# Dilated attention queries and keys kept in token order, with strided operands for the score products

## The chip, the cores and the metric

The kernel runs on one core of one Trainium2 chip. The metric is the device time of one launch in microseconds; three runs of the kernel before the change took 1457.19, 1458.5 and 1459.48 us (median 1458.5). All data is float32. "fp32r" in the profile is a float32 operand that TensorE takes in one pass; a plain float32 product shows as two MATMUL records.

## The reference, cut to what matters

The program is one encoder block: three attention mixers on the same normalised input, gates, and projections. The change touches only the first mixer, a dilated sliding-window attention with 24 heads of 64 in three groups of 8. The groups have dilations 1, 4 and 16:

```python
A_GROUPS = ((128, 1), (512, 4), (2048, 16))      # (window, dilation)
# per group: rope on q and k, then
def regroup(t):                                   # tokens t = u*dilation + r  ->  class r, place u
    return t.reshape(b, L, dilation, h, dh).transpose(0, 2, 1, 3, 4)
sc = einsum('znqhd,znkhd->znhqk', qb, kw) * dh ** -0.5      # within a class only
valid = abs(qpos - kpos) <= half                            # half = 64 places
p = exp(sc - m);  l = sum(p);  o = (p / l) @ v;  lse = m + log(l)
# the three groups' outputs are merged with softmax(lse) over the groups
```

A query sees only keys of its own residue class (token number modulo the dilation), up to 64 places away. In the third group a class has 1024 / 16 = 64 tokens, so it sees its whole class and no band is needed.

## The kernel before, in words

The program works in stages. The one that matters here is the dilated attention, from about 600 to 1030 us of the span. It handles 12 items, one for each pair of heads `p_` (0 to 3) and group `g` (0 to 2), in the order (0,0), (0,1), (0,2), (1,0) and so on.

**Projections.** `add_a` queues two dense units an item, one for the queries and one for the keys. `dense` (lines 143, 145, 147) does a unit as two halves of 512 tokens, 24 matmuls each. `rope_half` empties each half from PSUM: eight quarter multiplications for the rotated part and one full-width one on VectorE (lines 1049 and 1050 through `mult`), and then one addition on GpSimd (line 1056) that writes the rotated queries `aq` or keys `ak`. That addition also sorts: it reads `t1a` and `t2a` through `classes`, with a step of the dilation between elements, and writes through `half_of`, so that `aq` and `ak` hold whole residue classes one after the other.

**Attention of an item.** `scores` (line 1123) multiplies a tile of 128 queries by its window of keys for two heads, which lie on partitions 0 to 63 and 64 to 127. A call does four query tiles. A tile's window of keys has 192 or 256 columns in group 0, 192 in group 1, and 128 in group 2, where a tile holds two classes of 64 one after the other. `soft` adds a mask on VectorE (line 1135) and takes the exponential on ScalarE (lines 1138 to 1143); `trans` transposes on TensorE (lines 1160, 1169) and copies out on ScalarE (line 1172); `pv` (line 1186) multiplies by the values and writes the output `og` in order of tokens on ScalarE (line 1194); `stats` transposes the maxima and sums (line 1205), copies them to `sr` (lines 1208, 1210, 1212) and stores them to `std` in DRAM, for all three groups in the order of 16 classes. `values` loads the item's values from `vdr` into `vfull` (and `vpart`), with SyncE's DMA queue. When the three groups of a pair of heads are done, `combine` reads `std`, forms the weights, sends them through DRAM (`wgd`) and back broadcast (`wgt`), and multiplies `og` by them on VectorE (`weigh`, line 1334), with the sums over groups on GpSimd (line 1338).

**Order.** TensorE's order is written out by hand: `plan` lists the pieces of the current item between those of the last and the next, and `weave` mixes them with the dense matmuls of the item after the next by their costs in nanoseconds. In this stage the order on VectorE, ScalarE, GpSimd and SyncE is found by the framework's scheduler, from dependencies, priorities and its model of costs. Each engine then runs its instructions strictly in that order.

Of the kernel before, what the change touches and what calls it, by code (L numbers as in the profile page):

```python
# [10 lines left out]
AF = mybir.ActivationFunctionType  # L11
OP = mybir.AluOpType
# [3 lines left out]
S = 1024  # L16
# [2 lines left out]
EPS = 1e-6  # L19
HD = 64  # L20
DIL = (1, 4, 16)

C_ID, C_GP, C_GM, C_BM, C_END = 0, 130, 138, 146, 426
B_COS, B_SIN, B_QN, B_QS, B_KN, B_KS = 0, 512, 170, 234, 298, 362
# [26 lines left out]
def block(ctx: ExitStack, tc: tile.TileContext, x, xT, memT, cst, msk, bcst, tabA, gpost,  # L51
          wu, wv, wb, wmem, wbr, wout, out):
    nc = tc.nc
    V, A, G, PE = nc.vector, nc.scalar, nc.gpsimd, nc.tensor
# [390 lines left out]
    for k in range(8):  # L445
        if k % 2 == 0:
            load_wkv(k // 2)
        for e in range(2 if k == 0 else 1):
            t = slice(e * 512, e * 512 + 512) if k == 0 else slice(0, S)
# [206 lines left out]
    half = [slice(0, 512), slice(512, 1024)]  # L656
# [363 lines left out]
    with tc.tile_pool(name="aa", bufs=1, reuse_waits="tile") as aa:  # L1020
# [4 lines left out]
        vpart = aa.tile([P, 8, 2, 64], F32, name="avp")  # L1025
        G.memset(vpart, 0.0)

        def half_of(ap, half, g):

            if g == 0:  # L1030
                return ap[:, half * 512:half * 512 + 512]
            n = S // DIL[g] // 2
            return ap.rearrange("p (r u) -> p r u", r=DIL[g])[:, :, half * n:half * n + n]

        def classes(ap, g):
            return ap if g == 0 else ap.rearrange("p (u r) -> p r u", r=DIL[g])

        OPS = {}

        def rope_half(o, half, p, scale, g):  # L1040

            t = slice(half * 512, half * 512 + 512)
            t1 = ab.tile([P, 512], F32, name="t1a", bufs=3)
            t2 = ab.tile([P, 512], F32, name="t2a", bufs=3)
            cos, sin = tab[0][:, t], tab[1][:, t]

            def mult(out, x, y):
                if scale is None:
                    return V.tensor_tensor(out, x, y, op=OP.mult)  # L1049
                return V.scalar_tensor_tensor(out, x, scale, y, op0=OP.mult, op1=OP.mult)  # L1050

            for a in range(4):
                i, j = slice(32 * a, 32 * a + 32), slice(32 * (a ^ 1), 32 * (a ^ 1) + 32)
                mult(t2[i], p[j], sin[j])
            fp["last"] = mult(t1, p, cos)
            G.tensor_tensor(half_of(o, half, g), classes(t1, g), classes(t2, g), op=OP.add)  # L1056

        def add_a(p_, g):
            base = (p_ * 3 + g) * 2
            d = OPS[p_, g] = {}  # L1060

            def qk_evac(name, scale):
                def evac(half, p):
                    if half == 0:
                        d[name] = ab.tile([P, S], F32, name=f"a{name}", bufs=2)
                    rope_half(d[name], half, p, scale, g)
                return evac

            add_unit(wu[base], qk_evac("q", -0.125))
            add_unit(wu[base + 1], qk_evac("k", None))  # L1070

        def item(p_, g):
# [8 lines left out]
            def values():  # L1081

                v = vdr[g, p_]
                if g == 2:
                    vv = v.rearrange("(u r) f -> u r f", r=16)
                    for z in range(2):
                        nc.sync.dma_start(vfull[z * 64:z * 64 + 64].rearrange("p b h d -> p b (h d)"), vv[:, z::2])
                    return
                if g == 0:
                    nc.sync.dma_start(vfull[:, 0:7].rearrange("p b h d -> p b (h d)"),  # L1090
                                      v[64:960].rearrange("(b q) f -> q b f", q=128))
                else:
                    nc.sync.dma_start(vfull[:, 0:4].rearrange("p b h d -> p b (h d)"),
                                      v.rearrange("(u r) f -> u r f", r=4)[64:192])
                for z in range(2):
                    zs, f = slice(z * 64, z * 64 + 64), slice(z * 64, z * 64 + 64)
                    if g == 0:
                        nc.sync.dma_start(vpart[zs, 0:2, z], v.rearrange("(b q) f -> q b f", q=64)[:, 0::15, f])
                    else:
                        for e in range(2):  # L1100
                            nc.sync.dma_start(vpart[zs, e::2, z], v[768 * e:768 * e + 256].rearrange(
                                "(q r) f -> q r f", r=4)[:, :, f])
# [5 lines left out]
            def scores(b):  # L1108
                if b == 0:
                    d["ops"] = OPS.pop((p_, g))  # L1110
                    d["lx"] = aa.tile([P, 2, NT], F32, name="lxa", bufs=2)
                    d["sts"] = cb.tile([P, 2, 2, NT], F32, name="sts", bufs=2)
                qa, ka = d["ops"]["q"], d["ops"]["k"]
                for j in range(4):
                    T = 4 * b + j
                    lo, hi, _ = window(g, T)
                    n = hi - lo
                    if j % 2 == 0:
                        banks = [pss1(), pss1()]
                    raws[T] = [x[:, j % 2 * 256:j % 2 * 256 + n] for x in banks]  # L1120
                    for h in range(2):
                        hs = slice(h * 64, h * 64 + 64)
                        PE.matmul(raws[T][h], qa[hs, T * 128:T * 128 + 128], ka[hs, lo:hi], start=True, stop=True)  # L1123

            def soft(T):
                lo, hi, mo = window(g, T)
# [48 lines left out]
            def pv(b):  # L1175
                if b == 0:
                    d["og"] = OG[p_, g] = cb.tile([P, S], F32, name="og", bufs=4)
                og = d["og"]
                ov = pst().rearrange("p a b -> p (a b)")
                for j in range(4):  # L1180
                    terms = st.pop(4 * b + j)
                    n = len(terms[0])
                    for i in range(n):
                        for h in range(2):
                            (vt, x), z, pp = terms[h][i]
                            PE.matmul(ov[h * 64:h * 64 + 64, j * 128:j * 128 + 128], vt[:, x, z], pp,  # L1186
                                      start=i == 0, stop=i == n - 1)
                if g == 0:
                    dst, src = og[:, b * 512:b * 512 + 512], ov
                else:  # L1190
                    r = DIL[g] // 2
                    dst = og.rearrange("p (u r) -> p r u", r=DIL[g])[:, b * r:b * r + r]
                    src = ov.rearrange("p (r u) -> p r u", r=r)
                A.activation(dst, src, AF.Copy)

            def stats():
                sts, lx = d["sts"], d["lx"]
                for h in range(2):
                    if g == 1:
                        V.tensor_tensor(sts[:, h, 1, h::2], sts[:, h, 1, h::2], lx[:, h, h::2], op=OP.add)  # L1200
                    elif g == 0:
                        t = slice(7 * h, 7 * h + 1)
                        V.tensor_tensor(sts[:, h, 1, t], sts[:, h, 1, t], lx[:, h, t], op=OP.add)
                tp = pst()
                PE.transpose(tp[0:32, 0, :], sts.rearrange("p h s t -> p (h s t)"), ident)
                sr = cb.tile([32, 128], F32, name="sr", bufs=1)
                if g == 0:
                    A.activation(sr.rearrange("p (b a) -> p b a", b=16), tp[0:32, 0, :].rearrange("p (a b) -> p b a", b=16), AF.Copy)
                elif g == 1:
                    A.activation(sr.rearrange("p (b a) -> p b a", b=4), tp[0:32, 0, :].rearrange("p (a b) -> p b a", b=4), AF.Copy)  # L1210
                else:
                    A.activation(sr, tp[0:32, 0, :], AF.Copy)
                for h in range(2):
                    for q in range(2):
                        row = sr[(h * 2 + q) * 8:(h * 2 + q) * 8 + 8]
                        dst = std[p_, h, g, q]
                        if g == 0:
                            nc.sync.dma_start(dst.rearrange("(b t a) -> t b a", b=16, t=8),
                                              row.rearrange("p (b a) -> p b a", b=16))
                        elif g == 1:  # L1220
                            for f in range(2):
                                nc.sync.dma_start(dst.rearrange("(e r f a) -> f r e a", e=4, r=4, f=2)[f],
                                                  row[f:f + 7:2].rearrange("p (e a) -> p e a", e=4))
                        else:
                            nc.sync.dma_start(dst.rearrange("(t a) -> t a", t=8), row)

            size = [window(g, T)[1] - window(g, T)[0] for T in range(NT)]
            return dict(
# [525 lines left out]
def layout(inp):  # L1754
# [4 lines left out]
    r = {}  # L1759
# [37 lines left out]
    k = np.arange(256)[None]  # L1797
    m = np.zeros((P, 384), f)
    m[:, :256] = np.where(np.abs(p + 64 - k) <= 64, 0.0, 1e30)
    m[:, 256:] = np.where(p // 64 == k[:, :128] // 64, 0.0, 1e30)  # L1800
    r['msk'] = m
    cst[:, C_GP:C_GP + 8] = inp['g_pre'][0].reshape(8, P).T
    cst[:, C_GM:C_GM + 8] = inp['g_mem'][0].reshape(8, P).T
# [53 lines left out]
```

## Time and profile before

| quantity | value |
|---|---|
| median of three runs | 1458.5 us |
| the profiled execution, whole | 1458.88 us |
| its span in the profile | 1457.1 us |
| mean granted TensorE clock | 0.995 |
| TensorE matmul busy (PE) | 1423.2 us, 98% |
| VectorE busy (DVE) | 984.5 us, 68% |
| ScalarE busy (ACT) | 641.8 us, 44% |
| GpSimd busy (POOL) | 499.7 us, 34% |

A row of a group gives line, engine, operation, output<-input, shapes and count, then the busy time, the mean duration in nanoseconds, the idle time of that engine just before, and what ended it. A timeline row gives the start and the duration in microseconds, and in brackets the idle time before and its releaser; neighbouring instructions of a kind stand in one row. The ends of matmuls are modelled and overlap, so the time that a block of matmuls really takes is read from its start to the start of the next row. PEld are TensorE's weight loads. SPq is SyncE's queue.

### The profile page before, as it was taken

To read this page: it belongs to the slowest core of one execution; us is meant where nothing else is said; L and a number is where in the kernel's file an instruction comes from. 1 tells how busy PE (TensorE), PEld (TensorE's weight loads), DVE (VectorE), ACT (ScalarE), POOL (GpSimd) and SP (SyncE) were. 2 spreads that over 40 slices of the span, in tenths; PEclk is the share of its full clock that TensorE was granted. 3 is DMA by queue.
4 is the path that set the end of the run, shared out by engine and by line. 5 is a ranking of instruction groups with operands and counts; after the bars stand their busy time and mean duration, and the time that the engine had idled before them with its cause. 6 is when DMAs were issued, how large, how long until landed. Compare 5 with 4: busy or idle time off the path is not lost.

```text
span 1457.1 us, 20924 instructions
## 1 busy us (share of the span) xinstructions
PE 1423.2 (98%) x7548; PEld 1140.9 (78%) x7548; DVE 984.5 (68%) x1739; ACT 641.8 (44%) x1441; POOL 499.7 (34%) x382
## 2 busy tenths in 40 slices
PE   8999999999999999899999999999999999999998
PEld 7899986565666888687777778778787888888887
DVE  7665468776762367586687686873788787659643
ACT  6543365665554243145444544463534434212221
POOL 1415504666664420132232242230334331035322
PEclk9999999999999999999999999999999999999999
DMA  6332012232112675412131241342443443767122
GB/s 239 100 116 73 17 64 91 80 105 73 62 44 72 237 222 173 122 43 57 47 90 59 57 113 51 89 145 81 139 156 134 173 173 108 272 219 273 48 92 101
DMA packets 99448, 168.05 MB, mean 115 GB/s; under 512 B 21968, under 2 KB 51856, under 8 KB 99344
## 3 DMA queue, kind: packets, MB, share of 16 engines
q1 hardware_dynamic: 80192, 148.76, 31.7%
q10 hardware_dynamic: 19152, 17.96, 3.7%
q8 instruction: 59, 0.97, 0.3%
q14 instruction: 45, 0.37, 0.1%
HBM read 124.38 MB, written 42.30 MB: 114 GB/s over the span
## 4 chain that ended last, share of the span: by engine, by line
PE 76%; DVE 9%; ACT 5%; issue 5%; POOL 3%; DMA 2%; SPq 0%; ACTq 0%; POOLq 0%; DVEq 0%
PE s L125 9%; PE sc L125 9%; PE d L145 9%; PE d L143 8%; PE d L147 8%; PE s L967 6%; PE sc L1705 5%; PE ov L754 3%; PE d L967 2%; PE s L738 2%; PE tr L720 2%; PE s L739 2%; PE d L535 1%; PE tr L1186 1%; PE s L1123 1%
## 5 line engine op out<-in xcount | busy, mean ns | idle before, releaser
L143 PE MATMUL d<-hh,wh 128*128 128x512 f32 x672 | 271.2, 404 | 7.6 <-DVE t1a L1050 5.8
L147 PE MATMUL d<-hh,wl 128*128 128x512 f32 x672 | 269.4, 401 | 0.0
L145 PE MATMUL d<-hl,wh 128*128 128x512 f32 x672 | 269.4, 401 | 0.0
L105 ACT ACTIVATE wh<-wr 128x1024 fp32r<-128x1024 f32 (+1 forms) x79 | 72.2, 917 | 222.1 <-PE d L145 125.8
L143 PEld LDWEIGHTS d<-hh,wh 128*128 128x128 f32 x672 | 127.5, 190 | 38.0 <-issue 10.6
L145 PEld LDWEIGHTS d<-hl,wh 128*128 128x128 f32 x672 | 127.3, 189 | 31.3 <-issue 8.4
L147 PEld LDWEIGHTS d<-hh,wl 128*128 128x128 f32 x672 | 127.4, 190 | 29.1 <-issue 4.7
L745 POOL TENSOR_TENSOR bl<-bl,bp 128x512 f32<-128x512 f32 x96 | 131.5, 1370 | 53.6 <-ACT bp L741 48.1
L125 PE MATMUL sc<-hh,wh 128*128 128x512 f32 x384 | 118.4, 389 | 0.0
L106 DVE TENSOR_TENSOR wl<-wr,wh 128x1024 fp32r<-128x1024 f32 x53 | 74.6, 1409 | 37.5 <-ACT wh L105 37.1
L1056 POOL TENSOR_TENSOR aq<-t1a,t2a 128x512 f32<-128x512 f32 x24 | 44.7, 1862 | 160.7 <-DVE t1a L1050 149.4
L721 DVE TENSOR_REDUCE bn<-tr 128x1 f32<-128x512 f32 x128 | 86.1, 686 | 17.4 <-PE tr L720 16.1
L1049 DVE TENSOR_TENSOR t2a<-d,tab 32x512 f32<-32x512 f32 x96 | 66.0, 687 | 47.2 <-PE d L147 41.9
L741 ACT ACTIVATE bp<-s 128x512 f32<-128x512 f32 x128 | 75.9, 595 | 46.8 <-PE s L739 45.7
L1056 POOL TENSOR_TENSOR ak<-t1a,t2a 128x512 f32<-128x512 f32 x24 | 55.4, 2308 | 117.8 <-DVE t1a L1049 91.9
L125 PEld LDWEIGHTS sc<-hh,wh 128*128 128x128 f32 x384 | 72.1, 188 | 15.0
L1050 DVE SCALAR_TENSOR_TENSOR t2a<-d,tab 32x512 f32<-32x512 f32 x96 | 66.0, 687 | 25.8 <-PE d L147 24.0
L1432 POOL TENSOR_TENSOR sf<-wr 128x512 f32<-128x512 f32 x22 | 29.7, 1368 | 145.1 <-DVE ch L106 71.7
L1636 POOL TENSOR_TENSOR acc<-acc,th 128x1024 f32<-128x1024 f32 x15 | 40.9, 2729 | 112.0 <-DVE th L1635 109.3
L125 PE MATMUL sc<-hl,wh 128*128 128x512 f32 x192 | 74.7, 389 | 0.0
L1143 ACT ACTIVATE pra<-pra,sts 128x128 f32<-128x128 f32 (+2 forms) x152 | 66.4, 438 | 17.0 <-DVE sts L1135 17.0
L1135 DVE CUSTOM_DVE_ANT_0 pra<-s,mask 128x192 f32<-128x192 f32 (+2 forms) x192 | 56.1, 348 | 15.7 <-PE s L1123 14.9
(375 smaller groups left out, 3435.4 us busy)
## 6 DMA issues: line engine op xcount, KB each, us to landing
wr<-in_wu SPq DMA_DIRECT2D x64, 512.0 KB
th<-thd SPq DMA_DIRECT2D x24, 512.0 KB
thd<-rs ACTq DMA_DIRECT2D x44, 256.0 KB
g2d<-fth SPq DMA_DIRECT2D x24, 256.0 KB
vdr<-vr ACTq DMA_DIRECT2D x24, 256.0 KB
wgt<-wgd SPq DMA_DIRECT2D x24, 256.0 KB
ot<-od SPq DMA_DIRECT2D x12, 512.0 KB
wr<-in_wbr SPq DMA_DIRECT2D x24, 256.0 KB
```

The costliest lines, as they stand in the source:

```text
L105: A.activation(dst_h, src, AF.Copy)
L106: V.tensor_tensor(dst_l, src, dst_h.bitcast(F32), op=OP.subtract)
L125: PE.matmul(out_ps, a, b, start=i == 0, stop=i == n - 1)
L143: PE.matmul(dst, wh[:, k, :], hh[k][:, t], start=k == 0, stop=False)
L145: PE.matmul(dst, wh[:, k, :], hl[k][:, t], start=False, stop=False)
L147: PE.matmul(dst, wl[:, k, :], hh[k][:, t], start=False, stop=k == 7)
L721: fp["last"] = V.tensor_reduce(st[i]["n"][:, j, c:c + 1], s, axis=AX.X, op=OP.min)
L741: A.activation(pp, s, AF.Exp, scale=-1.0)
L745: G.tensor_tensor(lsum[i % 2], lsum[i % 2], pp, op=OP.add)
L967: PE.matmul(now[j], a, b, start=k == 0 and q == 0, stop=k == end and q == 2)
L1056: G.tensor_tensor(half_of(o, half, g), classes(t1, g), classes(t2, g), op=OP.add)
L1705: PE.matmul(parts[h], *terms[h][j], start=j == 0, stop=j == 23)
```

## The change

`aq` and `ak` are no longer sorted into classes. The GpSimd addition reads and writes contiguous rows, for all groups, and the score products take their operands with a step: 4 elements (16 bytes) in group 1, and 8 elements (32 bytes) in group 2, for the stationary queries as for the moving keys. In group 2 a step of 8 gives a tile of 128 tokens with the same number modulo 8, that is, the two classes T and T + 8 interleaved; the mask keeps the pairs whose places are both even or both odd, where before it kept the two diagonal squares of 64. The sizes of all products, masks and exponentials stay the same. The values of group 2 are loaded in that order too, with one DMA in place of two. Its output is written with a step of 8 in place of 16, and its statistics are brought to the order of 16 classes while they are copied to `sr` and stored.

```diff
+ORD = (1, 4, 8)
-        def half_of(ap, half, g):
+        def in_class(ap, g, a, b):
             if g == 0:
-                return ap[:, half * 512:half * 512 + 512]
-            n = S // DIL[g] // 2
-            return ap.rearrange("p (r u) -> p r u", r=DIL[g])[:, :, half * n:half * n + n]
-
-        def classes(ap, g):
-            return ap if g == 0 else ap.rearrange("p (u r) -> p r u", r=DIL[g])
+                return ap[:, a:b]
+            n = S // ORD[g]
+            assert b - a <= n - a % n
+            return ap.rearrange("p (u r) -> p r u", r=ORD[g])[:, a // n, a % n:a % n + b - a]
...
-            G.tensor_tensor(half_of(o, half, g), classes(t1, g), classes(t2, g), op=OP.add)
+            G.tensor_tensor(o[:, t], t1, t2, op=OP.add)
...
                 if g == 2:
-                    vv = v.rearrange("(u r) f -> u r f", r=16)
-                    for z in range(2):
-                        nc.sync.dma_start(vfull[z * 64:z * 64 + 64].rearrange("p b h d -> p b (h d)"), vv[:, z::2])
+                    nc.sync.dma_start(vfull.rearrange("p b h d -> p b (h d)"), v.rearrange("(q r) f -> q r f", r=8))
...
-                        PE.matmul(raws[T][h], qa[hs, T * 128:T * 128 + 128], ka[hs, lo:hi], start=True, stop=True)
+                        PE.matmul(raws[T][h], in_class(qa[hs], g, T * 128, T * 128 + 128), in_class(ka[hs], g, lo, hi), start=True, stop=True)
...
-                    r = DIL[g] // 2
-                    dst = og.rearrange("p (u r) -> p r u", r=DIL[g])[:, b * r:b * r + r]
+                    r = ORD[g] // 2
+                    dst = og.rearrange("p (u r) -> p r u", r=ORD[g])[:, b * r:b * r + r]
...
-                    A.activation(sr, tp[0:32, 0, :], AF.Copy)
+                    A.activation(sr.rearrange("p (j u) -> p j u", j=2), tp[0:32, 0, :].rearrange("p (u j) -> p j u", j=2), AF.Copy)
...
-                            nc.sync.dma_start(dst.rearrange("(t a) -> t a", t=8), row)
+                            nc.sync.dma_start(dst.rearrange("(j t u) -> t j u", j=2, t=8), row.rearrange("p (j u) -> p j u", j=2))
...
-    m[:, 256:] = np.where(p // 64 == k[:, :128] // 64, 0.0, 1e30)
+    m[:, 256:] = np.where(p % 2 == k[:, :128] % 2, 0.0, 1e30)
```

More of the change, by code (lines that the diff above doesn't have):

```diff
@@ L1026, in block, with rope_half @@
         G.memset(vpart, 0.0)
-        def half_of(ap, half, g):
+        def in_class(ap, g, a, b):
             if g == 0:
-                return ap[:, half * 512:half * 512 + 512]
-            n = S // DIL[g] // 2
-            return ap.rearrange("p (r u) -> p r u", r=DIL[g])[:, :, half * n:half * n + n]
-        def classes(ap, g):
-            return ap if g == 0 else ap.rearrange("p (u r) -> p r u", r=DIL[g])
+                return ap[:, a:b]
+            n = S // ORD[g]
+            assert b - a <= n - a % n
+            return ap.rearrange("p (u r) -> p r u", r=ORD[g])[:, a // n, a % n:a % n + b - a]
         OPS = {}
-        def rope_half(o, half, p, scale, g):
+        def rope_half(o, half, p, scale):
             t = slice(half * 512, half * 512 + 512)
@@ L1065, in evac @@
                         d[name] = ab.tile([P, S], F32, name=f"a{name}", bufs=2)
-                    rope_half(d[name], half, p, scale, g)
+                    rope_half(d[name], half, p, scale)
                 return evac
```

## The prediction

> **What bounds the kernel.** I read the busy table first, then the chain that ended last, then busy times by stretch, and then, for the dilated attention alone, the list of waits.
>
> ```profile
> PE 1423.2 (98%) x7548; PEld 1140.9 (78%) x7548; DVE 984.5 (68%) x1739; ACT 641.8 (44%) x1441; POOL 499.7 (34%) x382
> PE 76%; DVE 9%; ACT 5%; issue 5%; POOL 3%; DMA 2%; SPq 0%; ACTq 0%; POOLq 0%; DVEq 0%
> 600.00:1030.00 430.00, 422.46 (x2655) 339.51 (x2654) 303.77 (x726) 202.10 (x650) 119.33 (x58) 1.00 0.27 74
> PE tr L1205 <- ACT app L1172: 4.4, 6, 1.1
> PE tr L1160 <- ACT app L1172: 2.8, 4, 1.6
> ```
>
> TensorE bounds the kernel: it is busy 98% of the span, and in the stage of the change 422.5 of 430 us, with the clock granted in full. So an added microsecond of matmul costs a microsecond, unless it falls where TensorE would have stood still. Past the first dense unit, the waits there are only the two last rows, 4.4 + 2.8 = 7.2 us, both for ScalarE's copies `app`. No row names GpSimd or a DMA as TensorE's releaser. The change touches GpSimd, which is 28% busy there (119.33 of 430), and the score products, which are on TensorE. Everything hangs on what a step between elements costs TensorE.
>
> **Part 1: the score products.** The timeline gives three blocks with the start of the dense matmul that follows, and three dense starts in a row:
>
> ```profile
> 783.23 1.16 PE L1123 MATMUL s<-ak,aq 64*128 64x128 f32 x16
> 784.32 0.50 PE L143 MATMUL d<-hh,wh 128*128 128x512 f32 x1
> 748.77 1.57 PE L1123 MATMUL s<-ak,aq 64*128 64x192 f32 x16
> 750.27 0.50 PE L143 MATMUL d<-hh,wh 128*128 128x512 f32 x1
> 759.79 0.40 PE L143 MATMUL d<-hh,wh 128*128 128x512 f32 x1
> 760.02 0.39 PE L145 MATMUL d<-hl,wh 128*128 128x512 f32 x1
> 760.25 0.40 PE L147 MATMUL d<-hh,wl 128*128 128x512 f32 x1
> L1123 PEld LDWEIGHTS s<-ak,aq 64*128 64x128 f32 x384 | 29.4, 187 | 5.4 <-issue 4.5
> L1186 PEld LDWEIGHTS tr<-app,avs 128*64 128x64 f32 x480 | 26.7, 136 | 8.5 <-issue 8.5
> ```
>
> A block of group 2 (128 keys a tile) lasts 784.32 - 783.23 = 1.09 us, one of group 1 (192 keys) 750.27 - 748.77 = 1.50 us. A block has 16 records: 4 tiles, 2 heads, 2 records a product. If the two heads, which use different halves of the partitions, run side by side, 8 records follow one another, and the difference is 8 x 64 = 512 columns in 0.41 us: 0.80 ns a column. The rest, 1.09 - 1024 x 0.80 ns = 0.27 us, is the start of a block. The dense stream starts a matmul of 512 columns every 0.23 us, 0.45 ns a column. So a float32 score product takes its keys at little more than half the rate that TensorE can read contiguously. The weight loads give (187 - 136) / 64 = 0.80 ns a column of queries; 128 x 0.80 = 102 ns, just as long as the 128 columns that hide it.
>
> The trace shows no strided operand on TensorE, so the cost has to be bounded from other engines' rows, where the same step can be seen:
>
> ```profile
> 653.93 0.60 ACT L1194 ACTIVATE og<-tr 128x512 f32<-128x512 f32 x1 [1.08 <-PE tr L1186]
> 686.65 1.11 ACT L1194 ACTIVATE og<-tr 128x512 f32<-128x512 f32 x1 [1.08 <-PE tr L1186]
> 716.26 1.07 ACT L1194 ACTIVATE og<-tr 128x512 f32<-128x512 f32 x1 [0.20 <-PE tr L1186]
> L1143 ACT ACTIVATE pra<-pra,sts 128x128 f32<-128x128 f32 x64 | 24.9, 391 | 6.8 <-DVE sts L1135 6.8
> L1143 ACT ACTIVATE pra<-pra,sts 128x256 f32<-128x256 f32 x48 | 23.8, 498 | 6.5 <-DVE sts L1135 6.5
> 716.71 1.23 DVE L106 TENSOR_TENSOR wl<-wr,wh 128x1024 fp32r<-128x1024 f32 x1
> 751.52 2.01 DVE L1334 TENSOR_TENSOR og<-og,wgt 128x1024 f32<-128x1024 f32 x1
> L1135 DVE CUSTOM_DVE_ANT_0 pra<-s,mask 128x128 f32<-128x128 f32 x64 | 14.6, 286 | 2.1 <-PE s L1123 1.6 <-PE tr L1160 0.4
> L1135 DVE CUSTOM_DVE_ANT_0 pra<-s,mask 128x256 f32<-128x256 f32 x48 | 17.8, 420 | 13.4 <-PE s L1123 13.3
> ```
>
> The first three rows write `og` for groups 0, 1 and 2: contiguous, every 4th element, every 16th. ScalarE takes (498 - 391) / 128 = 0.84 ns a contiguous element; a step of 4 adds (1.11 - 0.60) / 512 = 1.00 ns, a step of 16 adds 0.92. So 1.8 ns an element, and 4 is as dear as 16. On VectorE, `weigh` reads one operand in steps where the split `wl` reads both contiguously: (2.01 - 1.23) / 1024 = 0.76 ns more, on (420 - 286) / 128 = 1.05, again 1.8 ns. Two engines with different contiguous rates come out at the same time for an element that has a 16-byte piece of memory to itself. The dense stream takes four elements, 16 bytes, in 4 x 0.45 = 1.8 ns. My reading is that SBUF delivers one such piece every 1.8 ns or a little less, to TensorE as well, and that keys at 0.80 ns a column cannot hide it.
>
> [...]
>
> The columns: group 1 has 8 blocks of 8 x 192 and group 2 has 8 blocks of 8 x 128, 12,288 + 8,192 = 20,480. The added price is 0.80 ns (exactly twice) at the low end, 1.00 at the high end (1.8 - 0.80), or nothing if TensorE hides it. I take 0.90, nearest to TensorE's own dense row: 18.4 us. A block begins with one load that nothing hides; at twice its 102 ns that is 16 x 0.10 = 1.6 us more (between nothing and this). Later loads, 215 ns at that rate, lie beside 128 columns of 218 ns. Sum on TensorE: +20.0 us.
>
> **Part 2: GpSimd's additions, and the stalls.** 32 of the 48 additions lose their step.
>
> ```profile
> 599.55 1.27 POOL L1056 TENSOR_TENSOR aq<-t1a,t2a 128x512 f32<-128x512 f32 x1 [51.77 <-DVE t1a L1050]
> 703.83 2.21 POOL L1056 TENSOR_TENSOR ak<-t1a,t2a 128x512 f32<-128x512 f32 x1 [4.36 <-DVE t1a L1049]
> 747.11 2.01 POOL L1056 TENSOR_TENSOR aq<-t1a,t2a 128x512 f32<-128x512 f32 x1 [3.76 <-PE d L147]
> 768.43 2.99 POOL L1056 TENSOR_TENSOR ak<-t1a,t2a 128x512 f32<-128x512 f32 x1 [3.69 <-DVE t1a L1049]
> 748.45 1.75 DVE L106 TENSOR_TENSOR wl<-wr,wh 128x1024 fp32r<-128x1024 f32 x1
> 770.51 2.79 DVE L1334 TENSOR_TENSOR og<-og,wgt 128x1024 f32<-128x1024 f32 x1
> 755.70 0.28 PE L1205 MATMUL tr<-cs,sts 128*32 128x128 f32 x1 [1.14 <-ACT app L1172]
> 775.37 0.44 PE L1160 MATMUL tr<-cs,pra 128*128 128x128 f32 x2 [0.51 <-ACT app L1172]
> 968.42 0.55 PE L1160 MATMUL tr<-cs,pra 128*128 128x128 f32 x3 [1.61 <-ACT app L1172]
> ```
>
> Contiguous additions (group 0) take 1.27 us, or 2.21 beside a VectorE instruction with two SBUF operands; sorting ones 2.01 and 2.99. Each saves 0.7 to 0.8 us, some 25 us of GpSimd in all. GpSimd is idle between, so nothing of that is on the path itself. But VectorE waits beside it: `wl` at 748.45 takes 1.75 against 1.23 us while the addition of 747.11 runs to 749.12, and `weigh` at 770.51 takes 2.79 against 2.01 us until the addition of 768.43 ends at 771.42. Those delays are handed on: VectorE's next masks, ScalarE's exponentials and `app`, TensorE's transposes at 755.70 (stall 1.14) and 775.37 (0.51). Both come once for each of three pairs of heads, the second as 1.61 at 968.42 the last time. Relief alone gives 3 x 0.5 + 2 x 0.5 + 0.8 = 3.3 us. Where these stalls shrink, what is late next is `weigh` itself, whose weights come by DMA.
>
> The same stalls also swallow part 1, since they follow the two group 1 blocks (748.77 and 767.47): TensorE comes later by some 8 x 192 x 0.90 ns = 1.4 us to transposes that wait for VectorE anyway. Relief and lateness together take them whole: 3 x 1.14 + 2 x 0.51 + 1.61 = 6.0 us. The remaining 1.2 of the 7.2 us I leave as they are.
>
> **Part 3: the rest, at nothing.** `values` for group 2 is one DMA in place of two on SyncE's queue, with rows of 4 KB in place of 512 bytes. It is issued at an item's fourth tile and needed at its first `pv`, four tiles later; without that cover its landing would stop `pv`, but no DMA stands among TensorE's releasers. The stores to `std` have runs of 256 bytes in place of 512; VectorE's first reader never waited for them:
>
> ```profile
> L1314 DVE TENSOR_TENSOR cmn<-cpt 128x16 f32<-128x16 f32 x3 | 0.5, 170 | 0.0
> L1212 ACT ACTIVATE sr<-tr 32x128 f32<-32x128 f32 x4 | 1.0, 255 | 0.8 <-PE tr L1205 0.8
> L1210 ACT ACTIVATE sr<-tr 32x128 f32<-32x128 f32 x4 | 1.0, 255 | 0.8 <-PE tr L1205 0.8
> ```
>
> Without that cover the weights would be late by the added landing time. The copy to `sr` becomes a sorting one like line 1210, at the same 255 ns. The output at a step of 8 lies between 1.07 and 1.11 us, on an engine less than half busy (202.10 of 430). The new mask changes values alone. The scheduler may order the other engines anew; no row prices that, and I bound it by three stalls of 1.14 us either way and take zero.
>
> **Sum.** 18.4 + 1.6 - 6.0 = +14.0 us on the profiled execution's 1458.88 us (span 1457.1 and 1.8 around it), which lies 0.4 above the median of 1458.5. Against the median: 1472.5 us, slower by 1.0%.
>
> **Rivals.**
> A step that costs TensorE nothing (faster). The score products use only half the rate of the dense stream, so TensorE's reader may have the time for a step; this decides where the price of an element is no more than 0.80 ns, and up to some 0.25 ns above that the stalls still pay for it. For it: 0.45 against 0.80. Against it: ScalarE, also slower than the dense stream, pays. Only the relief is left: -3.3, 1455.2 us.
> Only the loads are slow. 215 ns a load against 112 a record of group 2 and 161 of group 1: 64 x (103 + 54) ns = 10.0, plus 1.6 for first loads, less some 5.5 of stalls: +6, 1464.5 us.
> Four elements free. A step of 16 bytes costs nothing and 32 bytes does: 8,192 x 0.90 ns + 0.8 - 3.3 = +4.9, 1463.4 us. The two `og` rows speak against it. [...]
> Keys fetched twice a record (each record does half of a float32 product and may stream its keys twice, which would also explain 0.80 against 0.45): 3.6 ns a column, 20,480 x 2.8 ns = 57, less 7: +50, 1509 us.
>
> **How the numbers follow.** Chances: the forecast 0.53, no cost 0.30, loads alone 0.06, four elements free 0.05, fetched twice 0.06. The forecast's own range is 16.4 - 6.0 = +10 to 20.5 + 1.6 - 4 = +18 (stalls absorbed only in part), 1468 to 1477 us. About 0.2% (3 us) is what a measurement of this kernel can tell from no change. The no-cost rival's 3.3 us lies close to that: 0.19 of it faster, 0.11 within 0.2%. All others are slower: 0.70. Leaving the no-cost case out would leave 0.36 out, so the range reaches from 1454 to 1477 us.
>
> **What the profile after would show.** The score blocks: 3.0 us in place of 1.50 in group 1 and 2.1 in place of 1.09 in group 2 if I am right; unchanged if TensorE hides the step; 2.0 in both if the loads bind. The additions of line 1056 all near 1.3 us, or 2.2 beside VectorE. TensorE's waits for `app`: 7.2 us down to about 1. The prediction is wrong if the blocks keep their length, or if new waits of TensorE, of a reordered ScalarE or VectorE, take their place.

## The result, and the profile after

The changed kernel takes 1470.83 us (median of 4 runs, 1470.18 to 1471.37) against 1458.65 us before (median of 4): a ratio of 1.0084, 95% interval 1.0067 to 1.0102. The forecast was 1472.5 us, in a range of 1454 to 1477. The profiled execution took 1470.18 us with a span of 1468.4.

The busy table, the stretch of the dilated attention (busy microseconds of TensorE, its weight loads, VectorE, ScalarE and GpSimd, then the granted clock), the only wait that the list names for TensorE there, and one block of scores of each group with the dense matmul that follows it:

```profile
PE 1439.3 (98%) x7548; PEld 1156.5 (79%) x7548; DVE 975.6 (66%) x1739; ACT 644.8 (44%) x1441; POOL 473.8 (32%) x382
600.00:1043.00 443.00, 441.98 (x2661) 358.00 (x2661) 297.56 (x727) 205.99 (x651) 92.67 (x57) 1.00 0.26 73
PE tr L1202 <- ACT app L1169: 1.0, 3, 0.3
751.83 3.12 PE L1120 MATMUL s<-ak,aq 64*128 64x192 f32 x16
754.88 0.50 PE L144 MATMUL d<-hh,wh 128*128 128x512 f32 x1
787.03 2.28 PE L1120 MATMUL s<-ak,aq 64*128 64x128 f32 x16
789.24 0.50 PE L144 MATMUL d<-hh,wh 128*128 128x512 f32 x1
```

The score line is now 1120. A block of group 1 lasts 754.88 - 751.83 = 3.05 us where it lasted 1.50, a block of group 2 lasts 2.21 where it lasted 1.09. All eight blocks of a group last the same, 3.05 and 2.21 us, so that is 8 x 1.55 + 8 x 1.12 = 21.4 us more on TensorE. Its waits for `app` fell from 7.2 to 1.0 us, and the stage is now one unbroken stretch of TensorE, 441.98 of 443 us.

GpSimd's additions (line 1055 now), and VectorE beside them, at the places that the prediction showed:

```profile
749.31 1.29 POOL L1055 TENSOR_TENSOR aq<-t1a,t2a 128x512 f32<-128x512 f32 x1 [3.76 <-DVE t1a L1049]
771.43 2.20 POOL L1055 TENSOR_TENSOR ak<-t1a,t2a 128x512 f32<-128x512 f32 x1 [4.49 <-DVE t1a L1048]
751.51 1.22 DVE L107 TENSOR_TENSOR wl<-wr,wh 128x1024 fp32r<-128x1024 f32 x1
773.50 2.02 DVE L1331 TENSOR_TENSOR og<-og,wgt 128x1024 f32<-128x1024 f32 x1
```

The additions fell from 2.01 to 1.29 us and from 2.99 to 2.20, `wl` from 1.75 to 1.22, `weigh` from 2.79 to 2.02. The relief is there to the tenth of a microsecond.

How much of the 21.4 us the stalls swallowed is read from the starts of the first and the last score block, before and after:

```profile
626.93 0.43 PE L1123 MATMUL s<-ak,aq 64*128 64x192 f32 x2
999.81 1.16 PE L1123 MATMUL s<-ak,aq 64*128 64x128 f32 x16
```

```profile
625.26 0.43 PE L1120 MATMUL s<-ak,aq 64*128 64x192 f32 x2
1009.57 0.61 PE L1120 MATMUL s<-ak,aq 64*128 64x128 f32 x2
```

The distance grew from 372.9 to 384.3 us, by 11.4. Between the two starts lie eight blocks of group 1 and seven of group 2, 20.2 us of the added price. So 8.8 us went into time in which TensorE had stood still. 21.4 - 8.8 = 12.6 us, and the medians differ by 12.2. (The two profiled executions differ by 11.3 in span: the one before reached its first score block 626.93 - 625.26 = 1.7 us later. That was lost ahead of the changed stage. By the starts of the same instructions it fell behind by 1.2 us more between 54.7 and 57.2 us, where its granted clock was 0.51 and the other's 1.00, caught up with 0.9 us of it by 60.0 us, and was 1.5 us behind again at 603.1; from 596.6 to 603.4 us its granted clock was 0.50, and the other's 0.75 in the same stretch.) The order of instructions on TensorE, VectorE, ScalarE and GpSimd is the same in both traces, so none of it comes from the scheduler.

### The profile page after: what moved, and what is told of

The parts are those of the page before. It is cut to its first block, busy times and chain, and to the rows that moved or that the text cites. A ratio compares the mean times of both kernels' runs of the same rounds, so it can differ in the third digit from the quotient of the medians.

```text
span 1468.4 us, 20920 instructions
## 1 busy us (share of the span) xinstructions
PE 1439.3 (98%) x7548; PEld 1156.5 (79%) x7548; DVE 975.6 (66%) x1739; ACT 644.8 (44%) x1441; POOL 473.8 (32%) x382
## 4 chain that ended last, share of the span: by engine, by line
PE 80%; DVE 6%; ACT 4%; issue 4%; POOL 3%; DMA 2%; ACTq 0%; SPq 0%; POOLq 0%; DVEq 0%
PE d L146 9%; PE d L144 9%; PE d L148 9%; PE s L126 9%; PE sc L126 9%; PE s L968 6%; PE sc L1702 5%; PE s L1120 3%; PE ov L755 3%; PE tr L1183 2%; PE d L968 2%; PE s L739 2%; PE tr L721 2%; PE s L740 2%; PE d L536 2%
## 5 line engine op out<-in xcount | busy, mean ns | idle before, releaser
L1055 POOL TENSOR_TENSOR aq<-t1a,t2a 128x512 f32<-128x512 f32 x24 | 31.8, 1326 | 175.5 <-DVE t1a L1049 175.5
L1055 POOL TENSOR_TENSOR ak<-t1a,t2a 128x512 f32<-128x512 f32 x24 | 42.3, 1763 | 135.1 <-DVE t1a L1048 106.7
```

What stands on the lines that cost most here:

```text
L1055: G.tensor_tensor(o[:, t], t1, t2, op=OP.add)
```

## The experiments

The first theory is the one on record, the line theory: SBUF delivers a 16-byte piece every 1.8 ns, whoever reads, and that alone makes the time. Its rivals are that only the loads or only the keys pay, that the relief or another part of the change matters, and that the rule on TensorE is a different one.

**The relief alone** (`relief`):

```diff
         def in_class(ap, g, a, b):
-            if g == 0:
-                return ap[:, a:b]
...
+            return ap[:, a:b]
```

> The changed kernel with its contiguous GpSimd additions, but with score products that read contiguous slices for all groups (so groups 1 and 2 multiply the wrong tokens; sizes are unchanged). Line theory (a 16-byte piece of SBUF costs about 1.8 ns, whoever reads it): score blocks back at 1.50 us (group 1) and 1.09 us (group 2), and only the relief of VectorE is left: -3.3 us against the kernel before, 1455 us, TensorE's waits for app about 4 of the 7.2 us. Rival (the stalls go only because TensorE comes later): waits unchanged at 7.2 us, 1458.5 us.

Measured: 1454.54 us against 1458.17 us, ratio 0.9975 (0.9965 to 0.9984), that is 3.6 us faster. TensorE's waits in that trace:

```profile
PE tr L1198 <- ACT app L1165: 2.9, 6, 0.6
PE tr L1153 <- ACT app L1165: 1.1, 2, 0.9
```

They are 4.0 us where the kernel before had 7.2. The contiguous additions are worth what the prediction said, 3.6 us where it had 3.3, and VectorE shows them: `weigh` takes 2.01 us on average where it took 2.20, `wl` over the whole kernel 1.38 where it took 1.41. The rival falls: the waits shrink although all blocks of groups 1 and 2 last 1.50 and 1.09 us from start to start, as before, so that TensorE comes no later.

**The step alone** (`stride_only`): the kernel before, with

```diff
-PE.matmul(raws[T][h], qa[hs, T * 128:T * 128 + 128], ka[hs, lo:hi], start=True, stop=True)
+PE.matmul(raws[T][h], in_class(qa[hs], g, T * 128, T * 128 + 128), in_class(ka[hs], g, lo, hi), start=True, stop=True)
```

> The kernel before, with its sorting additions on GpSimd, but score products that read with the step of 4 and 8 elements (so they multiply the wrong tokens in groups 1 and 2). The price of the step without the relief. Line theory: blocks 3.05 and 2.21 us as in the changed kernel, +21.4 us of TensorE; its lateness alone swallows nearly all of the stalls, so 1471 to 1473 us, and the relief is worth nothing once the step is paid. If the relief was needed for the stalls to go: 1474 to 1476 us.

Measured: 1471.0 us, ratio 1.0089 (1.0075 to 1.0103), the blocks of 3.05 and 2.21 us, and of TensorE's waits one row is left:

```profile
PE tr L1213 <- ACT app L1180: 1.0, 3, 0.3
```

That is the changed kernel's time without its relief. Once TensorE arrives that much later, nearly all of the stalls are gone whether VectorE is relieved or not: compared start by start with the kernel before, 8.3 us of standing still went here and 8.8 in the changed kernel. The two effects overlap, they don't add up.

**All but the step** (`both_sorted`): the changed kernel with the sorting addition put back, for the residues modulo 4 and 8.

```diff
-            G.tensor_tensor(o[:, t], t1, t2, op=OP.add)
+            if g and name in 'qk':
+                G.tensor_tensor(half_of(o, half, g), classes(t1, g), classes(t2, g), op=OP.add)
+            else:
+                G.tensor_tensor(o[:, t], t1, t2, op=OP.add)
```

> The changed kernel with both queries and keys sorted by the GpSimd addition again (by residue modulo 4 and modulo 8), so that the score products read contiguously; the pairing of classes T and T + 8, its values, mask, output and statistics stay. All theories in which the operands' step is the whole cost: 1458.5 us within 1.5, blocks 1.50 and 1.09 us. If the values' DMA, the sorting copy of the statistics or the stores cost something: above 1460 us.

Measured: 1458.57 us against 1458.17, ratio 1.0002 (0.9993 to 1.0011). The pairing of classes T and T + 8, the one DMA of values, the output at a step of 8, the sorted copy of the statistics and their shorter runs in DRAM together cost nothing that can be measured.

**Keys only and queries only** (`k_only`, `q_only`): the other operand is sorted by the addition, as above, and read contiguously.

> The changed kernel with the queries (the stationary operand) sorted by the GpSimd addition and only the keys (the moving operand) read with a step. Line theory: the stream of keys pays by itself, blocks of about 2.95 us in group 1 and 2.1 us in group 2 (only the unhidden first load gets cheaper, 0.1 us). If the loads were the cost: 1.50 and 1.09 us. If the loads bind in group 2 alone (240 ns measured a record there, 1.87 ns a column against 1.79 in group 1): group 2 falls to 8 x 128 x 1.79 ns + 0.27 = 2.1 us, group 1 stays.

> The changed kernel with the keys sorted by the GpSimd addition and only the queries (the stationary operand) read with a step. Line theory: a load of 128 columns at 1.8 ns takes 230 ns, longer than the 162 and 112 ns of contiguous keys beside it, so both groups get blocks of 8 x 230 ns + 0.37 = 2.2 us. If loads read from SBUF in another way: 1.50 and 1.09 us, at most 0.1 more.

One run each gave 1467.72 and 1464.89 us, beside 1457.6 for the kernel before on the same chip. The blocks, first with a step in the keys alone, then in the queries alone:

```profile
751.65 2.97 PE L1131 MATMUL s<-ak,aq 64*128 64x192 f32 x16
754.55 0.50 PE L144 MATMUL d<-hh,wh 128*128 128x512 f32 x1
786.55 2.11 PE L1131 MATMUL s<-ak,aq 64*128 64x128 f32 x16
788.60 0.50 PE L144 MATMUL d<-hh,wh 128*128 128x512 f32 x1
```

```profile
750.10 2.19 PE L1131 MATMUL s<-ak,aq 64*128 64x192 f32 x16
752.22 0.50 PE L144 MATMUL d<-hh,wh 128*128 128x512 f32 x1
784.05 2.17 PE L1131 MATMUL s<-ak,aq 64*128 64x128 f32 x16
786.15 0.50 PE L144 MATMUL d<-hh,wh 128*128 128x512 f32 x1
```

With strided keys 2.90 and 2.05 us: nearly all of the price by themselves. With strided queries 2.12 and 2.10, the same for both groups although the one has 192 columns a record and the other 128, while the mean load of the score products grew from 187 to 280 ns. So here the loads set the pace: (2.10 - 0.37) / 8 = 216 ns a load by the prediction's arithmetic for the start of a block (read from the starts of the records themselves, past the first pair, it is 0.23 to 0.24 us). So both operands pay, and the two don't add up: the step costs a block of group 1 1.40 us in the keys, 0.62 in the queries and 1.55 in both, a block of group 2 0.96, 1.01 and 1.12.

**A step of three** (`step3`):

```diff
-            return ap.rearrange("p (u r) -> p r u", r=ORD[g])[:, a // n, a % n:a % n + b - a]
+            return ap[:, 0:1023].rearrange("p (u r) -> p r u", r=3)[:, a // 128 % 3, 0:b - a]
```

> The changed kernel with a step of 3 elements (12 bytes) for queries and keys of groups 1 and 2 (wrong tokens, same sizes). Line theory: three quarters of a piece an element, 1.35 ns a column, blocks of 2.4 us (group 1) and 1.75 us (group 2). If a step costs from 16 bytes on only: 1.50 and 1.09 us. If any step over 8 bytes costs the same: 3.05 and 2.21 us.

```profile
750.24 2.38 PE L1118 MATMUL s<-ak,aq 64*128 64x192 f32 x16
752.54 0.50 PE L144 MATMUL d<-hh,wh 128*128 128x512 f32 x1
784.30 1.73 PE L1118 MATMUL s<-ak,aq 64*128 64x128 f32 x16
785.96 0.50 PE L144 MATMUL d<-hh,wh 128*128 128x512 f32 x1
```

2.30 and 1.66 us, between the contiguous blocks and those at a step of 4, and near the 2.4 and 1.75 expected. The price grows with the step, in group 1 from 1.50 us contiguous over 2.30 at 12 bytes to 3.05 at 16: in these products it goes by the size of the step and not only by whether there is one. The whole kernel took 1461.93 us in its one run.

**Dense projections with a step** (`dense_step`): the one-pass matmuls, to see the same price where a contiguous element takes 0.45 ns.

```diff
+        def mv(x):
+            m = step // 2
+            return x[:, t] if step == 1 else x.rearrange("p (u r) -> p r u", r=step)[:, half * m:half * m + m]
+        def st(x, k):
+            return x.rearrange("p k f -> p (k f)").rearrange("p (f r) -> p r f", r=8)[:, k] if wstep else x[:, k, :]
...
+            how = {4: dict(step=2), 6: dict(step=4), 8: dict(wstep=True)}.get(p_ * 3 + g, {})
```

> The kernel before with single dense projections changed (wrong tokens or weights there, same sizes): in item 4 the moving operand has a step of 2 elements, in item 6 of 4, in item 8 the stationary operand has a step of 8. These are one-pass products at 0.44 ns a column. Line theory (an absolute time for each 16-byte piece): 512 columns take 0.46 us at step 2 and 0.92 us at step 4, against 0.23; with strided weights they stay at 0.23 to 0.24, since a load of 230 ns hides behind the stream. Rival (a step halves the rate, whatever it is): 0.45 us at step 4, and 0.23 or 0.45 at step 2.

Two starts each with a step of 2, with a step of 4, and with strided weights:

```profile
716.54 0.63 PE L153 MATMUL d<-hh,wh 128*128 128x512 f32 x1
716.99 0.63 PE L155 MATMUL d<-hl,wh 128*128 128x512 f32 x1
...
785.36 0.66 PE L153 MATMUL d<-hh,wh 128*128 128x512 f32 x1
785.82 0.66 PE L155 MATMUL d<-hl,wh 128*128 128x512 f32 x1
...
856.78 0.40 PE L153 MATMUL d<-hh,wh 128*128 128x512 f32 x1
857.02 0.41 PE L155 MATMUL d<-hl,wh 128*128 128x512 f32 x1
```

0.45 us at a step of 2, but 0.46 and not 0.92 at a step of 4: here the line theory is wrong by a factor of two, and the rival's halving holds. Strided weights cost almost nothing (0.24 us from start to start against 0.23), although the median record of a load grew from 188 to 327 ns: beside 512 columns hardly any of that shows.

**What is different about the score products** (`apart_step`, `apart_flat`, `dense_f32`). They are plain float32, two records a product, and two heads run at a time: in the block of 748.77 of the kernel before, records start in pairs, 7 ns apart, and a pair every 0.16 us. Either the two heads take turns at fetching, or a float32 record itself asks twice as much. `apart_step` takes the heads one after the other, and `apart_flat` does so on `relief`:

```diff
+                order = [(h, j) for h in range(2) for j in range(4)] if g else [(h, j) for j in range(4) for h in range(2)]
+                for h, j in order:
```

> The changed kernel, but in groups 1 and 2 a block multiplies all four tiles of the first head and then all four of the second, so that the two heads no longer run side by side. Shared theory (TensorE fetches a 16-byte piece in some 0.9 ns, and the two heads take turns): a column costs 0.9 ns for one head alone, 16 records x 192 x 0.9 ns = 2.8 us in group 1 and 1.85 us in group 2 plus the start, no dearer than side by side (3.05 and 2.21). Twice theory (a float32 record streams its keys twice): 1.8 ns a column for one head alone, 5.5 and 3.7 us plus the start. One piece every 1.8 ns: the same 5.5 and 3.7 us.

> The same order of heads on the kernel with contiguous operands (wrong tokens in groups 1 and 2), as the measure for the one before. If the heads ran side by side, the blocks double: 16 x 192 x 0.80 ns + 0.3 = 2.75 us and 16 x 128 x 0.80 + 0.3 = 1.95 us. If they took turns on TensorE already: 1.50 and 1.09 us.

Their blocks of group 1, with the step and without:

```profile
765.03 4.69 PE L1122 MATMUL s<-ak,aq 64*128 64x192 f32 x16
769.65 0.56 PE L144 MATMUL d<-hh,wh 128*128 128x512 f32 x1
765.57 0.87 PE L1122 MATMUL s<-ak,aq 64*128 64x192 f32 x2
765.91 0.86 PE L1122 MATMUL s<-ak,aq 64*128 64x192 f32 x2
```

```profile
749.28 2.32 PE L1118 MATMUL s<-ak,aq 64*128 64x192 f32 x16
751.53 0.50 PE L144 MATMUL d<-hh,wh 128*128 128x512 f32 x1
```

Contiguous, the block grows from 1.50 to 2.25 us; it doesn't double. That is the time of 12 of the 16 records one after the other, 12 x 0.16 + 0.27 = 2.2 us by 0.16 us a record and the prediction's start of a block, so by this estimate four still run beside others. With the step it takes 4.62 us, and in the part where one head runs alone a record of 192 columns starts every 765.91 - 765.57 = 0.34 us, 1.8 ns a column. Two heads side by side took (3.05 - 0.27) / (8 x 192) = 1.81 ns. One head alone pays as much as two. They don't take turns. (The whole kernels took 1513.71 and 1462.35 us in one run each; why the first lost so much more than its blocks is told at the end.)

`dense_f32` does single dense projections in plain float32 over all partitions, and one in one pass with a step of 8:

```diff
+            if f32:
+                x = x.bitcast(F32)
...
+            how = {4: dict(f32=True), 6: dict(f32=True, step=4), 8: dict(f32=True, step=2), 10: dict(step=8)}.get(p_ * 3 + g, {})
```

> The kernel before with single dense projections taken as plain float32 (two records a product), over all 128 partitions and with nothing beside them: item 4 contiguous, item 6 with a step of 4 elements, item 8 with a step of 2; item 10 one-pass with a step of 8 elements (wrong tokens with a step, same sizes). Contiguous: 512 x 0.83 ns = 0.43 us a record. Shared theory: 0.46 us a record at step 4 and at step 2. Twice theory: 0.92 us at step 4 and 0.46 at step 2. One-pass, step 8: 0.46 us as at step 4 if a fetch costs 0.9 ns, 0.92 if 32 bytes cost more than 16.

Two starts each: contiguous, a step of 4, a step of 2 (rows of two records), and one pass with a step of 8:

```profile
707.53 1.02 PE L155 MATMUL d<-hh,wh 128*128 128x512 f32 x2
708.39 1.02 PE L157 MATMUL d<-hl,wh 128*128 128x512 f32 x2
...
847.65 1.98 PE L155 MATMUL d<-hh,wh 128*128 128x512 f32 x2
849.45 1.98 PE L157 MATMUL d<-hl,wh 128*128 128x512 f32 x2
...
960.07 1.06 PE L159 MATMUL d<-hh,wl 128*128 128x512 f32 x2
960.97 1.06 PE L155 MATMUL d<-hh,wh 128*128 128x512 f32 x2
...
1044.04 0.62 PE L157 MATMUL d<-hl,wh 128*128 128x512 f32 x1
1044.47 0.62 PE L159 MATMUL d<-hh,wl 128*128 128x512 f32 x1
```

A plain float32 record of 512 columns takes 0.43 us contiguous, 0.45 at a step of 2 and 0.90 at a step of 4; a one-pass record takes 0.23, 0.45, 0.46 and, at a step of 8, 0.43. In nanoseconds a column:

| step in elements | 1 | 2 | 4 | 8 |
|---|---|---|---|---|
| one pass (fp32r) | 0.45 | 0.88 | 0.90 | 0.84 |
| plain float32 record | 0.84 | 0.88 | 1.76 | not measured alone |

So at a step of 4 it is the float32 record that takes twice as long as a one-pass record, and not the pair of heads; at a step of 2 both take 0.88. (With the dearer dense projections in them, `dense_step` took 1479.76 us and `dense_f32` 1604.4.)

**Half a sort** (`pairs`, `pairs_write`). If two neighbouring elements are kept together, a class has a step of 2, where the table shows plain float32 to be nearly free (0.88 ns a column against 0.84), while GpSimd moves runs of 8 bytes.

```diff
+            r = a // n
+            return ap.rearrange("p (a u b) -> p a b u", a=ORD[g] // 2, b=2)[:, r // 2, r % 2, a % n:a % n + b - a]
...
+                n = 512 // ORD[g]
+                x, y = [z.rearrange("p (u a b) -> p a u b", a=ORD[g] // 2, b=2) for z in (t1, t2)]
+                G.tensor_tensor(pairs_of(o, g)[:, :, half * n:half * n + n], x, y, op=OP.add)
```

> The changed kernel, but the GpSimd addition half-sorts: it moves runs of two neighbouring elements, so that a class has a step of 2 elements (8 bytes) in the queries and keys, for groups 1 and 2. Line theory: two elements of a 16-byte piece are used, 1.8 / 2 = 0.9 ns against 0.80 ns a column, so the blocks cost 1.50 to 1.65 us (group 1) and 1.09 to 1.2 us (group 2), the additions stay near 1.3 us, and the kernel comes out at 1455 to 1457 us, a little under the kernel before. Rival (any step costs TensorE double): 3.0 and 2.2 us, 1471 us. If GpSimd pays for the pairs: additions of 2.0 us and no relief, 1458 to 1460 us.

`pairs_write` reads `t1` and `t2` in their order and moves the pairs in the output only:

```diff
-                G.tensor_tensor(pairs_of(o, g)[:, :, half * n:half * n + n], x, y, op=OP.add)
+                x, y = [z.rearrange("p (u a b) -> p u a b", a=ORD[g] // 2, b=2) for z in (t1, t2)]
+                G.tensor_tensor(pairs_of(o, g)[:, :, half * n:half * n + n].rearrange("p a u b -> p u a b"), x, y, op=OP.add)
```

> The half-sorting kernel, with the addition reading both inputs in their order and moving the pairs in its one output instead of its two inputs. If GpSimd pays for each operand that is not contiguous: additions of 1.3 to 1.5 us (group 1 and 2, queries) in place of 1.6, TensorE's waits for app at or a little under the 3.8 us of the half-sorting kernel, 1455.5 us against 1456.1. If a write in pairs costs as much as two reads: the same as the half-sorting kernel.

`pairs` takes 1456.07 us against 1458.17, ratio 0.9986 (0.9977 to 0.9994); `pairs_write` takes 1454.83 against 1457.97, ratio 0.998 (0.997 to 0.9989). Both beat the kernel before and the changed one. The additions of groups 1 and 2 and a block of group 1, in `pairs_write`:

```profile
L1064 POOL TENSOR_TENSOR ak<-t1a,t2a 128x512 f32<-128x512 f32 x16 | 28.5, 1779 | 89.4 <-DVE t1a L1052 61.1 <-DVE sts L1209 28.3
L1064 POOL TENSOR_TENSOR aq<-t1a,t2a 128x512 f32<-128x512 f32 x16 | 21.6, 1349 | 76.4 <-DVE t1a L1053 76.4
747.83 1.64 PE L1129 MATMUL s<-ak,aq 64*128 64x192 f32 x16
749.39 0.50 PE L144 MATMUL d<-hh,wh 128*128 128x512 f32 x1
```

The block takes 1.56 us, 0.06 over the contiguous one, and the additions are as short as contiguous ones (1349 ns for the queries on average; in `pairs`, with two inputs in pairs, 1596, so there GpSimd did pay a part of the sort). All of the relief is kept for some 0.06 x 16 = 1.0 us of TensorE.

## Why the prediction was right, point by point

**What bounds.** Right. TensorE's time decided, and what was added outside the stalls came through: 12.6 us by the starts, 12.2 by the medians. The range of 1454 to 1477 us was wide enough to hold a free step too (1455.2), so it is the lengths of the blocks, and not a time inside the range, that bear the forecast out.

**The price of the step.** Right in size: 18.4 + 1.6 = 20.0 us forecast, 21.4 measured; blocks of 3.0 and 2.1 us forecast, 3.05 and 2.21 measured. `stride_only` and `both_sorted` show that it is the whole cause. The keys by themselves bring 8 x 1.40 + 8 x 0.96 = 18.9 us of it (`k_only`); the last 2.5 come only with the queries' step, 0.15 us a block where 0.10 was put down for a first load. `q_only` shows that loads alone would set the pace at about the forecast 215 ns (which was worked loosely: twice 102 is 204 ns, and 102 + 128 x 0.9 is 217). That leaves nothing of the rivals of slow loads alone and of four free elements: a step of four elements doubled the blocks of group 1 just as a step of eight doubled those of group 2. The reason given for the price was only half right. "SBUF delivers one such piece every 1.8 ns or a little less, to TensorE as well" does not hold: a one-pass product at a step of 4, with a new 16 bytes for every element, takes 0.90 ns a column. The figure fitted because the score products are plain float32, which took 1.76 ns a column at that step (`dense_f32`) and had no part in the working of the 1.8 ns: the right size was in part luck. The piece of 16 bytes itself was the reading of the prediction; the runs show times by step, and no piece. That the dense stream takes a contiguous 16 bytes in 1.8 ns proved nothing about pieces.

**The rival of keys fetched twice.** It was given 3.6 ns a column, from the same wrong 1.8 ns a piece. With 0.9 ns an element its doubling gives the 1.8 ns that was measured at a step of 4. A second pass over the whole row does not fit, though: at a step of 2 it would make 2 x 0.88 ns of a record that takes 0.88. Each key fetched twice in a row would fit; that is not shown.

**The relief.** Right: 3.3 us forecast, 3.6 measured in `relief`, and handed on as described.

**The stalls.** The right stalls went, and their size was too small: 6.0 us forecast, 8.8 measured. The term summed the idle time in TensorE's rows. Those count from the modelled end of a matmul, but a dense matmul makes way for the next after 0.23 us, not 0.40. From start to start the stall before 755.70 is 755.70 - 754.16 - 0.23 = 1.31 us and not 1.14, by the row of the kernel before that stands ahead of it:

```profile
754.16 0.40 PE L145 MATMUL d<-hl,wh 128*128 128x512 f32 x1
```

Compared start by start with the trace after, the six stalls of the forecast come to 7.0 us. The other 1.8 us are shorter waits with little or no idle time in their rows, most of them at the transposes just behind; the transpose at 757.23, for one, has 0.10 us there and followed its predecessor 0.26 us sooner after the change. And the lateness did not need the relief for this: by `stride_only` it swallows 8.3 us alone. The size of the term made the forecast 2.8 us too high, where the price of the step made it 1.4 too low.

**The rest at nothing.** Right, by `both_sorted`, and the scheduler left the order alone.

## What to carry to other kernels

A step of 3, 4 or 8 elements was not free on TensorE: the score blocks took 2.30 us at 3 and 3.05 at 4 in place of 1.50, and 2.21 at 8 in place of 1.09. Before moving a sort from an idle engine into the operands of the engine that bounds the kernel, measure one block at that step, moving and stationary operand each: what is saved elsewhere counts only where it reaches the bound, here 3.6 us (`relief`) of the 26 by which GpSimd's busy time fell (499.7 to 473.8). A half-sort that leaves two neighbours together can serve both engines; here it gained 0.2%. And measure stalls of a matmul stream from start to start.

## What the runs showed of the hardware that I had not expected

One-pass matmuls ran at half their rate for any step tried (0.88, 0.90 and 0.84 ns a column at 2, 4 and 8 elements, against 0.45), while plain float32 records lost 5% at a step of 2 (0.88 against 0.84) and half their rate at a step of 4 (1.76). That a float32 record reads each element twice in a row would fit these numbers (by an estimate from the table 16 bytes would then cost 0.9 ns for one read, 1.8 for two or four, and 3.4 for eight), but no run here shows it, and that part stays open.

`apart_step` lost 43 us on the changed kernel, of which its longer blocks make up 8 x 1.57 + 8 x 1.15 = 22 (group 2 took 3.36 us). TensorE's waits in its stage were the same 1.0 us, but the granted clock, the figure behind the five busy times, fell to 0.95 where it had been 1.00:

```profile
600.00:1090.00 490.00, 488.98 (x2677) 398.02 (x2676) 300.10 (x730) 213.52 (x657) 92.55 (x57) 0.95 0.23 68
```

5% of 490 us is 24 us, by that estimate enough for the other 21. The clock was not low throughout. Behind 13 of the 16 strided blocks it was 0.50 for 3.4 or 6.8 us, beginning between 1.5 us before and 0.4 us after the end of the block. Inside the block of 765.03 it was 1.00, so the 1.8 ns a column above is a figure of the full clock; the block of 674.62 ran its last 1.45 us at 0.50 and lasted the same 4.62 us:

```profile
765.03:769.65 4.62, 4.62 (x18) 3.87 (x16) 3.71 (x11) 2.64 (x11) 0.00 (x0) 1.00 0.92 239
677.79:679.24 1.45, 1.45 (x5) 0.90 (x4) 0.92 (x6) 0.90 (x5) 0.00 (x0) 0.50 0.97 314
```

It was not tried why. One head at a time is not enough for it, since `apart_flat` kept a clock of 1.00 in this stage; nor is the step with two heads side by side, at 1.00 in the changed kernel. This is one execution, and the cause stays open.

On GpSimd an addition with two contiguous inputs and an output in runs of 8 bytes took 1349 ns on average (`pairs_write`), a wholly contiguous one in the changed kernel 1326:

```profile
L1055 POOL TENSOR_TENSOR aq<-t1a,t2a 128x512 f32<-128x512 f32 x24 | 31.8, 1326 | 175.5 <-DVE t1a L1049 175.5
```
